# The head of a hybrid layer kernel: order of x, of the transposes and of the first two projection units

## Chip, cores and metric

The kernel runs on one core of one Trainium2 chip. The metric is device microseconds of one execution; the kernel before took 150.55 us as the median of three runs (150.08 to 150.64).

## What is computed

One DeepNorm layer over x of 256 rows and 1024 columns in float32. A first LayerNorm gives h. One projection takes h (1024 columns) to the inputs of four mixers (Mamba-2, HGRN2, retention, block attention); each mixer gives 256 columns, gated; an output projection takes their concatenation back to 1024 columns; a second LayerNorm takes 2^0.25 times h plus the result.

```python
h = _layernorm(x, emb_ln_g, emb_ln_b)
proj = einsum('bld,dn->bln', h, w_in)
q, f_raw, i, gate = the HGRN2 columns of proj
f = lb + (1 - lb) * sigmoid(f_raw)
...
y = einsum('blm,md->bld', y_cat, w_out)
out = _layernorm(2 ** 0.25 * h + y, ln_g, ln_b)
```

Only the head is touched here: the first LayerNorm, the transposition of h, and the projections `h_f` (the `f_raw` columns) and `h_q` (the `q` columns), with `h_i` behind them.

## The kernel before

**Layout.** x lies in two tiles of 128 rows, `xt0` and `xt1`. The normalised rows `xn` are transposed by TensorE in 16 blocks of 128 x 128 (8 column slices k, two row tiles T); slice k of both tiles shares one PSUM bank, and `h_in(k)` (line 307) evicts it with the LayerNorm's gain and bias, per partition, from the small table `ch`.

**Three products for one.** Every float32 operand is split into a high part, rounded to float32r by a cast (`whi`, `hhi`), and the rest (`wlo`, `hlo`, a subtraction on VectorE). A projection is the sum of hi x hi, hi x lo and lo x hi. `split_hi` (line 218) casts a weight tile on ScalarE, `split_lo` (line 227) makes its rest on VectorE. A unit is a group of 256 (or 260) columns; its weights come as two tiles j of four slices each, 512 KB a tile, so a unit is 8 slices x 3 products x 2 halves = 48 matmuls of 256 columns.

**Order.** The schedule is written out by hand: each engine executes its instructions in the order in which the program lists them, and waits where an input is not there. SP issues all loads in the order of the `load_w` calls (line 193); the tiles come from a ring of five buffers (`raw`), and a load into a buffer waits until `split_lo` has read what was in it. The mixers' steps are hung onto slots, two per unit: `begin(slot)` (line 1064) issues the load of three units ahead, the cast of two units ahead, the mixers' steps of the slot and the low part of two units ahead; then `project(slot)` issues the matmuls.

**The head, in its order.** SP: four half tiles of x (lines 159 to 162), the identity matrix out of the constants (line 165), the first unit's tile 0 in two pieces, `ch` (line 237), tile 1 in two pieces, the other constants, the second unit, two small tables, the third unit. TensorE: three matmuls on a tile of zeros (`WARM`, line 178). VectorE: statistics of each half tile (`ln_stats`, line 265), `ln_scale` (line 268: mean and variance, epsilon, and on POOL the power of -1/2), `lnb` = -mean x scale (line 288), which ScalarE's way of normalising takes as its bias. `ln_apply` (line 273) normalises in halves: three on VectorE, one on ScalarE. TensorE transposes slices 0 to 3 of tile 0, then of tile 1; `h_in` evicts them. `first_unit` (line 337) transposes one further slice ahead of each of its first four steps and multiplies slice by slice: hi x hi of slice k, then hi x lo of slice k - 1. The h_q unit's hi products come behind (`project(2, (0, 1))`), then the first unit's products with the low weights, then the second half of h_q, and in slots 2 and 3 its products with the low weights. Slot 4 is the first of `h_i`. `hgrn_gate` and `hgrn_key` (slots 0 and 1) take `h_f`, `hgrn_query` (slot 4) takes `h_q`.

`ldec` and `mm` (lines 714, 715) are two tiles of 1024 columns of the Mamba-2 mixer, which are free until its scores are made.

Of the kernel before, what the change touches and what calls it, by code (L numbers as in the profile page):

```python
# [17 lines left out]
P = 128  # L18
# [104 lines left out]
def hybrid_layer(  # L123
# [35 lines left out]
    for T in range(NT):  # L159
        for hf in range(2):  # L160
            nc.sync.dma_start(xt[T][:, hf * 512:hf * 512 + 512],
                              x[T * P:(T + 1) * P, hf * 512:hf * 512 + 512])
    ch = cp.tile([P, C_FREE], F32, name="ch")
    ck = cp.tile([P, K_FREE], F32, name="ck")
    nc.sync.dma_start(ck[:, :P], consts[:, :P])
# [6 lines left out]
    nc.gpsimd.memset(mhalf, -0.5)  # L172

# [4 lines left out]
    for _ in range(WARM):  # L178
        nc.tensor.matmul(wb, warm[:, :P], warm, start=True, stop=True)  # L179
# [13 lines left out]
    def load_w(i, j, parts=1):  # L193
# [10 lines left out]
        t = wp.tile(shape, F32, tag="raw", bufs=5, name=f"wr_{name}_{j}")  # L204
# [31 lines left out]
    load_w(0, 0, 2)  # L236
    nc.sync.dma_start(ch, chan)
    load_w(0, 1, 2)
    nc.sync.dma_start(ck[:, P:], consts[:, P:])
    for j in range(2):  # L240
        load_w(1, j)
# [4 lines left out]
    for j in range(2):  # L246
        load_w(2, j)
# [12 lines left out]
    lnb = sb([P, 1], "lnb")  # L260
# [7 lines left out]
    def ln_scale(T):  # L268
        nc.vector.bn_aggr(lmv[T], lst[T])
        (nc.gpsimd, nc.vector)[T].tensor_scalar(lrs[T], lmv[T][:, 1:2], LN_EPS, None, op0=ALU.add)  # L270
        nc.gpsimd.tensor_tensor(lrs[T], lrs[T], mhalf[:, :1], op=ALU.pow)

    def ln_apply(T, hf):
        cs = slice(hf * 512, hf * 512 + 512)
        if (T, hf) == (0, 1):
            nc.scalar.activation(xn[T][:, cs], xt[T][:, cs], AF.Identity, scale=lrs[T][:, 0:1],
                                 bias=lnb[:, 0:1])
            return
        nc.vector.tensor_scalar(xn[T][:, cs], xt[T][:, cs], lmv[T][:, 0:1], lrs[T][:, 0:1],  # L279
                                op0=ALU.subtract, op1=ALU.mult)  # L280

    ln_stats(0, 0)
    ln_stats(0, 1)
    ln_stats(1, 0)
    ln_scale(0)
    ln_stats(1, 1)
    ln_scale(1)
    nc.vector.scalar_tensor_tensor(lnb, lmv[0][:, 0:1], -1.0, lrs[0], op0=ALU.mult, op1=ALU.mult)
    split_hi(0, 0, 2, (0,))
    for hf in range(2):  # L290
        for T in range(NT):
            ln_apply(T, hf)
    split_hi(0, 0, 2, (1,))
    split_lo(0, 0, 2, (0,))
# [3 lines left out]
    trb = {}  # L298

    def h_transpose(k, T):  # L300
        if T == 0:
            trb[k] = bank(f"tr{k}")
        nc.tensor.transpose(trb[k][:, T * P:(T + 1) * P], xn[T][:, k * P:(k + 1) * P], ident)  # L303

    hfs = {}

    def h_in(k):
        hf = hfs[k] = sb([P, SEQ], f"hf{k}", tag="hf", bufs=4)
        g, b = ch[:, C_EG + k:C_EG + k + 1], ch[:, C_EB + k:C_EB + k + 1]
        if k == 0:  # L310
            nc.scalar.activation(hhi[:, k, :], trb[k][:, :SEQ], AF.Identity, scale=g, bias=b)
            nc.vector.tensor_scalar(hf, trb[k][:, :SEQ], g, b, op0=ALU.mult, op1=ALU.add)
            return
        nc.scalar.activation(hf, trb[k][:, :SEQ], AF.Identity, scale=g, bias=b)
        if k == KT - 1:
            nc.scalar.copy(hhi[:, k, :], hf)
        else:
            nc.vector.tensor_copy(hhi[:, k, :], hf)
# [818 lines left out]
```

## Time and profile before

| | before |
|---|---|
| median of three runs | 150.55 us |
| the profiled execution | 150.44 us |
| its span in the trace | 148.7 us |
| outside the span | 1.74 us |
| mean granted TensorE clock | 0.976 |
| TensorE busy | 136.5 us, 92% |
| VectorE busy | 116.6 us, 78% |
| ScalarE busy | 75.1 us, 50% |

Times in the trace run from the span's start. In its rows PE is TensorE's matmuls and PEld its weight loads (one ahead of each matmul), DVE is VectorE, ACT ScalarE, POOL GpSimd, and SPq the queue from which SP issues its DMAs. A row names the line, the operation, output<-inputs and the shapes; in brackets it says how long the engine was idle before it and what ended that. A float32 matmul or transpose stands in the trace as one record or as two.

### The profile page before, as it was taken

What the parts mean: (1) busy time and instruction counts of PE and PEld (TensorE: products, weight loads), DVE (VectorE), ACT (ScalarE), POOL (GpSimd) and SP (SyncE); (2) the same over time, 40 slices, a digit from 0 to 9 for tenths busy, and PEclk for the clock granted to TensorE, in tenths of its full rate; (3) what the DMA queues carried; (4) which work ended last, traced back from release to release, by engine and by line L of the source; (5) the groups of instructions that cost most, each with busy time, mean ns of one, the idle gap of its engine ahead of it and who ended that gap; (6) DMA issues with size and microseconds to landing.
All of it is one profiled execution on the core that took longest, in us unless ns stands there. A gap on an engine that the chain in (4) does not pass through costs nothing.

```text
span 148.7 us, 3074 instructions
## 1 busy us (share of the span) xinstructions
PE 136.5 (92%) x1224; PEld 122.2 (82%) x1224; DVE 116.6 (78%) x241; ACT 75.1 (50%) x122; POOL 17.8 (12%) x23
## 2 busy tenths in 40 slices
PE   5669999999999999999999999999999999999800
PEld 3159999999999998878899999999888888888800
DVE  2689977999596397969997599976969995378681
ACT  3079967752451859599709970054576635000000
POOL 4230000000000000000061018014002200004040
PEclk9969999999999999999999999999999999999995
DMA  4899289999858331694625820179773550000304
GB/s 157 265 387 361 68 283 363 294 294 356 228 156 253 129 84 57 156 267 163 179 86 145 315 110 4 35 238 382 247 233 93 180 155 0 0 0 0 141 0 141
DMA packets 9533, 26.05 MB, mean 175 GB/s; under 512 B 1072, under 2 KB 1968, under 8 KB 9264
## 3 DMA queue, kind: packets, MB, share of 16 engines
q1 hardware_dynamic: 9088, 25.35, 52.4%
q10 hardware_dynamic: 432, 0.52, 1.0%
q8 instruction: 9, 0.15, 0.4%
q14 instruction: 4, 0.03, 0.1%
HBM read 24.82 MB, written 1.05 MB: 174 GB/s over the span
## 4 chain that ended last, share of the span: by engine, by line
PE 82%; DVE 8%; DMA 3%; ACT 1%; SPq 1%; POOLq 1%; issue 1%; POOL 1%; DVEq 0%
PE pj_gg L381 8%; PE po L993 5%; PE po L994 5%; PE po L992 5%; PE pj_h_f L346 4%; PE pj_xs L420 4%; PE pj_m_k L420 4%; PE pj_m_g L420 4%; PE pj_r_k L420 4%; PE pj_m_q L420 4%; PE pj_h_i L420 4%; PE pj_zv L381 4%; PE pj_h_q L420 4%; PE pj_r_v L420 4%; PE pj_r_q L420 4%; DMA xt<-in_x_dram 3%
## 5 line engine op out<-in xcount | busy, mean ns | idle before, releaser
L992 PE MATMUL po<-whi_wo,yhi 128*128 128x512 f32 (+1 forms) x40 | 14.0, 350 | 0.0
L993 PE MATMUL po<-wlo_wo,yhi 128*128 128x512 f32 (+1 forms) x40 | 14.0, 349 | 0.0
L994 PE MATMUL po<-whi_wo,ylo 128*128 128x512 f32 (+1 forms) x40 | 13.9, 348 | 0.0
L225 ACT CAST whi_wo<-wr_wo 128x1024 fp32r<-128x1024 f32 x8 | 8.2, 1049 | 4.0 <-DMA wr_wo<-in_wo_dram 2.8
L234 DVE TENSOR_TENSOR wlo_wo<-wr_wo,whi_wo 128x1024 fp32r<-128x1024 f32 x8 | 9.6, 1218 | 0.0
L710 POOL TENSOR_SCALAR_AFFINE_SELECT ra<-ahi 128x1024 fp32r<-128x1024 f32 x1 | 1.1, 1101 | 64.5 <-DVE ahi L706 64.5
L992 PEld LDWEIGHTS po<-whi_wo,yhi 128*128 128x128 f32 x40 | 7.5, 188 | 1.1
L993 PEld LDWEIGHTS po<-wlo_wo,yhi 128*128 128x128 f32 x40 | 7.5, 188 | 1.0
L994 PEld LDWEIGHTS po<-whi_wo,ylo 128*128 128x128 f32 x40 | 7.5, 188 | 1.0
L225 ACT CAST whi_zv<-wr_zv 128x1024 fp32r<-128x1024 f32 x4 | 4.2, 1047 | 6.8 <-PE pj_xs L420 3.4
L656 DVE SCALAR_TENSOR_TENSOR cacc_xs<-pj_xs,ch,cacc_xs 128x255 f32<-128x255 f32 (+2 forms) x6 | 2.9, 482 | 4.7 <-ACT cacc_xs L654 4.6
L381 PE MATMUL pj_zv<-whi_zv,hhi 128*128 128x512 f32 x16 | 6.5, 406 | 0.0
L1000 DVE TENSOR_TENSOR xn<-xn,po 128x512 f32<-128x512 f32 (+1 forms) x5 | 2.9, 580 | 4.4 <-PE po L994 4.4
L381 PE MATMUL pj_gg<-whi_gg,hhi 128*128 128x512 f32 x16 | 6.4, 398 | 0.0
L381 PE MATMUL pj_zv<-whi_zv,hlo 128*128 128x512 f32 x16 | 6.3, 394 | 0.0
L381 PE MATMUL pj_gg<-whi_gg,hlo 128*128 128x512 f32 x16 | 6.3, 394 | 0.0
L381 PE MATMUL pj_zv<-wlo_zv,hhi 128*128 128x512 f32 x16 | 6.3, 392 | 0.0
L381 PE MATMUL pj_gg<-wlo_gg,hhi 128*128 128x512 f32 x16 | 6.3, 392 | 0.0
L303 PE MATMUL tr<-ck,xn 128*128 128x128 f32 x16 | 3.8, 384 | 2.6 <-DVE xn L279 2.6
L179 PE MATMUL warm<-warm 128*128 128x512 f32 x6 | 4.5, 914 | 1.5 <-DVE warm L176 1.5
L303 PEld LDWEIGHTS tr<-ck,xn 128*128 128x128 f32 x16 | 2.7, 197 | 3.7 <-DVE xn L279 3.7
L225 ACT CAST whi_gg<-wr_gg 128x1024 fp32r<-128x1024 f32 x4 | 4.2, 1045 | 2.5 <-DMA wr_gg<-in_w_dram 1.7
(281 smaller groups left out, 490.7 us busy)
## 6 DMA issues: line engine op xcount, KB each, us to landing
wr_wo<-in_wo_dram SPq DMA_DIRECT2D x8, 512.0 KB, 3.8
wr_zv<-in_w_dram SPq DMA_DIRECT2D x4, 512.0 KB, 4.7
rb<-in_rows_dram SPq DMA_DIRECT2D x2, 1024.0 KB, 7.1
wr_gg<-in_w_dram SPq DMA_DIRECT2D x4, 512.0 KB, 4.7
wr_h_i<-in_w_dram SPq DMA_DIRECT2D x2, 520.0 KB, 4.9
xt<-in_x_dram SPq DMA_DIRECT2D x4, 256.0 KB, 3.8
wr_h_f<-in_w_dram SPq DMA_DIRECT2D x4, 256.0 KB, 5.2
wr_h_q<-in_w_dram SPq DMA_DIRECT2D x2, 512.0 KB, 5.6
```

The source lines that it names most:

```text
L179: nc.tensor.matmul(wb, warm[:, :P], warm, start=True, stop=True)
L225: copy(whi[i, j][:, r, :], t[:, r, :])
L234: nc.vector.tensor_sub(wlo[i, j][:, r, :], t[:, r, :], whi[i, j][:, r, :].bitcast(F32))
L303: nc.tensor.transpose(trb[k][:, T * P:(T + 1) * P], xn[T][:, k * P:(k + 1) * P], ident)
L346: nc.tensor.matmul(ps[n], l[:, n * P:(n + 1) * P], r[:, k, :], start=(k == 0 and q == 0), stop=(k == KT - 1 and q == 2))
L381: nc.tensor.matmul(ps_of[name, T], l[:, k, ts], r, start=(k == 0 and q == 0), stop=(k == KT - 1 and q == 2))
L420: nc.tensor.matmul(ps, l, r, start=(n == 0), stop=(n == len(seq) - 1))
L656: nc.vector.scalar_tensor_tensor(a_[:, d:], ps[:, :SEQ - d], tap(3 - d), a_[:, d:], op0=ALU.mult, op1=ALU.add)
L992: nc.tensor.matmul(po[T, c0], yhi[:, k, ts], hi, start=(i == 0 and j == 0), stop=False)
L993: nc.tensor.matmul(po[T, c0], yhi[:, k, ts], lo, start=False, stop=False)
L994: nc.tensor.matmul(po[T, c0], ylo[:, k, ts], hi, start=False, stop=(i == 3 and j == 1))
L1000: nc.vector.tensor_add(xn[T][:, cs], xn[T][:, cs], po[T, cs.start])
```

## The change

The first row tile of x is loaded in halves as before, the second as one transfer of whole rows, and `ch` is issued from ScalarE's queue ahead of everything. The identity is made on POOL instead of loaded. Both tiles' scales are computed on VectorE with POOL's power; `lnb` stands between the statistics of the second tile's halves. ScalarE normalises all of tile 0 in two halves, VectorE all of tile 1 in four quarters. TensorE transposes all eight slices of tile 0, then runs one more matmul on zeros (`keep_warm(1)`), then six slices of tile 1. Two slices now share a bank.

`first_units` multiplies the units h_f and h_q side by side, slice by slice, h_q one slice behind, and then both with their low weights. The weight casts of both units are placed between the evictions by a table (`CASTS`). The first unit's weights lie in the mixer tiles `mm` and `ldec` instead of the ring. The loads' order is both units' tile 0, both units' tile 1, the third unit, then constants and tables. Casts and low parts of the third unit move to slot 0, all ahead of `hgrn_key`.

```diff
@@ -156,13 +156,12 @@
     xt = [sb([P, DM], f"xt{T}") for T in range(NT)]
-    for T in range(NT):
-        for hf in range(2):
-            nc.sync.dma_start(xt[T][:, hf * 512:hf * 512 + 512],
-                              x[T * P:(T + 1) * P, hf * 512:hf * 512 + 512])
     ch = cp.tile([P, C_FREE], F32, name="ch")
+    nc.scalar.dma_start(ch, chan)
+    for T, st in ((0, 512), (1, DM)):
+        for c in range(0, DM, st):
+            nc.sync.dma_start(xt[T][:, c:c + st], x[T * P:(T + 1) * P, c:c + st])
     ck = cp.tile([P, K_FREE], F32, name="ck")
-    nc.sync.dma_start(ck[:, :P], consts[:, :P])
     ident = ck[:, K_ID:K_ID + P]
     tri = ck[:, K_TRI:K_TRI + P]
     one2 = ck[:, K_ONE2:K_ONE2 + 2]
@@ -170,13 +169,23 @@
     mhalf = cp.tile([P, 8], F32, name="mhalf")
     nc.gpsimd.memset(mhalf, -0.5)
+    nc.gpsimd.memset(ident, 1.0)
+    nc.gpsimd.affine_select(out=ident, in_=ident, pattern=[[1, P]], compare_op=ALU.is_equal, fill=0.0,
+                            base=0, channel_multiplier=-1)
+
+    lnb = sb([P, 1], "lnb")
+    nc.scalar.copy(lnb, mhalf[:, 0:1])
     warm = sb([P, 512], "warm", tag="att")
     nc.vector.memset(warm, 0.0)
     wb = bank("warm")
-    for _ in range(WARM):
-        nc.tensor.matmul(wb, warm[:, :P], warm, start=True, stop=True)
+
+    def keep_warm(n):
+        for _ in range(n):
+            nc.tensor.matmul(wb, warm[:, :P], warm, start=True, stop=True)
+
+    keep_warm(WARM)
     e1 = sb([P, 2, SEQ], "e1")
     nc.gpsimd.memset(e1, 0.0)
@@ -201,7 +210,9 @@
             b = int(name[2:])
             shape = [P, 2, 512]
             src = wo[:, 2 * b:2 * b + 2, j * 512:j * 512 + 512]
-        t = wp.tile(shape, F32, tag="raw", bufs=5, name=f"wr_{name}_{j}")
+
+        t = (sb(shape, f"wr_{name}_{j}", tag=("mm", "ldec")[j]) if i == 0 else
+             wp.tile(shape, F32, tag="raw", bufs=5, name=f"wr_{name}_{j}"))
         st = shape[1] // parts
         for q in range(parts):
             r = slice(q * st, (q + 1) * st)
@@ -233,18 +244,16 @@
             r = slice(q * st, (q + 1) * st)
             nc.vector.tensor_sub(wlo[i, j][:, r, :], t[:, r, :], whi[i, j][:, r, :].bitcast(F32))
-    load_w(0, 0, 2)
-    nc.sync.dma_start(ch, chan)
-    load_w(0, 1, 2)
+    for j in range(2):
+        for i in range(2):
+            load_w(i, j)
+    for j in range(2):
+        load_w(2, j)
     nc.sync.dma_start(ck[:, P:], consts[:, P:])
-    for j in range(2):
-        load_w(1, j)
     lev = cp.tile([P, 5, 64], I32, name="lev")
     nc.sync.dma_start(lev, lev_tab)
     rw = cp.tile([P, R_SMALL], F32, name="rw")
     nc.sync.dma_start(rw, rows[:, 0:R_SMALL].to_broadcast([P, R_SMALL]))
-    for j in range(2):
-        load_w(2, j)
     def row(n):
         o, c = ROFF[n]
@@ -267,55 +275,57 @@
     def ln_scale(T):
         nc.vector.bn_aggr(lmv[T], lst[T])
-        (nc.gpsimd, nc.vector)[T].tensor_scalar(lrs[T], lmv[T][:, 1:2], LN_EPS, None, op0=ALU.add)
+        nc.vector.tensor_scalar(lrs[T], lmv[T][:, 1:2], LN_EPS, None, op0=ALU.add)
         nc.gpsimd.tensor_tensor(lrs[T], lrs[T], mhalf[:, :1], op=ALU.pow)
-
-    def ln_apply(T, hf):
-        cs = slice(hf * 512, hf * 512 + 512)
-        if (T, hf) == (0, 1):
-            nc.scalar.activation(xn[T][:, cs], xt[T][:, cs], AF.Identity, scale=lrs[T][:, 0:1],
-                                 bias=lnb[:, 0:1])
-            return
-        nc.vector.tensor_scalar(xn[T][:, cs], xt[T][:, cs], lmv[T][:, 0:1], lrs[T][:, 0:1],
-                                op0=ALU.subtract, op1=ALU.mult)
     ln_stats(0, 0)
     ln_stats(0, 1)
+    ln_scale(0)
     ln_stats(1, 0)
-    ln_scale(0)
+    nc.vector.scalar_tensor_tensor(lnb, lmv[0][:, 0:1], -1.0, lrs[0], op0=ALU.mult, op1=ALU.mult)
     ln_stats(1, 1)
     ln_scale(1)
-    nc.vector.scalar_tensor_tensor(lnb, lmv[0][:, 0:1], -1.0, lrs[0], op0=ALU.mult, op1=ALU.mult)
-    split_hi(0, 0, 2, (0,))
-    for hf in range(2):
-        for T in range(NT):
-            ln_apply(T, hf)
-    split_hi(0, 0, 2, (1,))
-    split_lo(0, 0, 2, (0,))
+    for c in range(0, DM, 512):
+        nc.scalar.activation(xn[0][:, c:c + 512], xt[0][:, c:c + 512], AF.Identity,
+                             scale=lrs[0][:, 0:1], bias=lnb[:, 0:1])
+    for c in range(0, DM, 256):
+        nc.vector.tensor_scalar(xn[1][:, c:c + 256], xt[1][:, c:c + 256], lmv[1][:, 0:1],
+                                lrs[1][:, 0:1], op0=ALU.subtract, op1=ALU.mult)
+    split_hi(0, 0, 2)
     hhi = cp.tile([P, KT, SEQ], F32R, name="hhi")
     hlo = cp.tile([P, KT, SEQ], F32R, name="hlo")
-    trb = {}
+
+    trp = [bank(f"tr{j}").rearrange("p (k t) -> p k t", k=2) for j in range(5)]
+    trb = [trp[(k + 1) // 2][:, (k + 1) % 2, :] for k in range(KT)]
     def h_transpose(k, T):
-        if T == 0:
-            trb[k] = bank(f"tr{k}")
         nc.tensor.transpose(trb[k][:, T * P:(T + 1) * P], xn[T][:, k * P:(k + 1) * P], ident)
+    for k in range(KT):
+        h_transpose(k, 0)
+    keep_warm(1)
+    for k in range(6):
+        h_transpose(k, 1)
     hfs = {}
+    CASTS = {1: ((1, 0), (0,)), 4: ((0, 1), (0,)), 5: ((0, 1), (1,)), 6: ((1, 1), (0,)),
+             7: ((1, 1), (1,))}
+
     def h_in(k):
-        hf = hfs[k] = sb([P, SEQ], f"hf{k}", tag="hf", bufs=4)
+        hf = hfs[k] = sb([P, SEQ], f"hf{k}", tag="hf", bufs=6)
         g, b = ch[:, C_EG + k:C_EG + k + 1], ch[:, C_EB + k:C_EB + k + 1]
+        t = trb[k]
         if k == 0:
-            nc.scalar.activation(hhi[:, k, :], trb[k][:, :SEQ], AF.Identity, scale=g, bias=b)
-            nc.vector.tensor_scalar(hf, trb[k][:, :SEQ], g, b, op0=ALU.mult, op1=ALU.add)
+            nc.scalar.activation(hhi[:, k, :], t, AF.Identity, scale=g, bias=b)
+            nc.vector.tensor_scalar(hf, t, g, b, op0=ALU.mult, op1=ALU.add)
             return
-        nc.scalar.activation(hf, trb[k][:, :SEQ], AF.Identity, scale=g, bias=b)
-        if k == KT - 1:
-            nc.scalar.copy(hhi[:, k, :], hf)
-        else:
-            nc.vector.tensor_copy(hhi[:, k, :], hf)
+        nc.scalar.activation(hf, t, AF.Identity, scale=g, bias=b)
+        if k in CASTS:
+            split_hi(*CASTS[k][0], 2, CASTS[k][1])
+        nc.vector.tensor_copy(hhi[:, k, :], hf)
+        if k == 3:
+            split_hi(1, 0, 2, (1,), nc.vector.tensor_copy)
         h_rest(k - 1)
         if k == KT - 1:
             h_rest(k)
@@ -323,49 +333,40 @@
     def h_rest(k):
         nc.vector.tensor_sub(hlo[:, k, :], hfs[k], hhi[:, k, :].bitcast(F32))
-    for k in range(4):
-        h_transpose(k, 0)
-    for k in range(4):
-        h_transpose(k, 1)
-    for k in range(4):
+    for k in range(6):
         h_in(k)
-    split_hi(0, 1, 2, (0,))
     ps_of, hq = {}, {}
-    def first_unit():
-
-        ps = [bank(f"pj_h_f{n}")[:, :SEQ] for n in range(2)]
-        ps_of["h_f", 0], ps_of["h_f", 1] = ps
-
-        def part(k, q):
-            l = (whi, whi, wlo)[q][0, k // 4][:, k % 4]
+    def first_units():
+
+        ps = [[bank(f"pj_{names[i]}{n}")[:, :SEQ] for n in range(2)] for i in range(2)]
+        for n in range(2):
+            ps_of["h_f", n], hq[n] = ps[0][n], ps[1][n]
+
+        def part(i, k, q):
+            l = (whi, whi, wlo)[q][i, k // 4][:, k % 4]
             r = (hhi, hlo, hhi)[q]
             for n in range(2):
-                nc.tensor.matmul(ps[n], l[:, n * P:(n + 1) * P], r[:, k, :], start=(k == 0 and q == 0),
-                                 stop=(k == KT - 1 and q == 2))
-        for k in range(KT):
-            if k < 4:
-                h_transpose(k + 4, 0)
-                h_transpose(k + 4, 1)
-                h_in(k + 4)
-            if k == 1:
-                split_hi(0, 1, 2, (1,), nc.vector.tensor_copy)
-            part(k, 0)
-            if k:
-                part(k - 1, 1)
-        part(KT - 1, 1)
-        split_lo(0, 0, 2, (1,))
-        split_lo(0, 1, 2)
-        split_hi(1, 0)
-        split_hi(1, 1)
-        project(2, (0, 1))
-        for k in range(KT):
-            part(k, 2)
-        project(3, (0, 1))
-
-    def project(slot, parts=(0, 1, 2)):
+                nc.tensor.matmul(ps[i][n], l[:, n * P:(n + 1) * P], r[:, k, :],
+                                 start=(k == 0 and q == 0), stop=(k == KT - 1 and q == 2))
+        for k in range(KT + 2):
+            for i, d, q in ((0, 0, 0), (0, 1, 1), (1, 1, 0), (1, 2, 1)):
+                if 0 <= k - d < KT:
+                    part(i, k - d, q)
+            if k == 0:
+                for k_ in (6, 7):
+                    h_transpose(k_, 1)
+                for k_ in (6, 7):
+                    h_in(k_)
+        for i in range(2):
+            for j in range(2):
+                split_lo(i, j)
+            for k in range(KT):
+                part(i, k, 2)
+
+    def project(slot):
         i, j = divmod(slot, 2)
         name = names[i]
@@ -384,14 +385,11 @@
         def wk(k):
             hi = whi[i, k // 4][:, k % 4]
-            return hi, wlo[i, k // 4][:, k % 4] if 2 in parts else hi
+            return hi, wlo[i, k // 4][:, k % 4]
         if name in CHAN:
-            if name == "h_q":
-                if j not in hq:
-                    hq[j] = bank(f"pj_h_q{j}")[:, :SEQ]
-            elif j == 0:
+            if j == 0:
                 ps_of[name] = pp.tile([P, 2, SEQ], F32, tag="pp", name=f"pj_{name}")
-            ps = hq[j] if name == "h_q" else ps_of[name][:, j, :]
+            ps = ps_of[name][:, j, :]
             cs = slice(j * P, (j + 1) * P)
             def trip(k):
@@ -412,12 +410,11 @@
                 hi, lo = wk(k)
                 return (hhi[:, k, ts], hi), (hlo[:, k, ts], hi), (hhi[:, k, ts], lo)
         seq = [(k, q) for k in range(KT) for q in range(3)]
-        if slot < 4:
+        if slot < 6:
             seq.sort(key=lambda kq: kq[1] == 2)
         for n, (k, q) in enumerate(seq):
-            if q in parts:
-                l, r = trip(k)[q]
-                nc.tensor.matmul(ps, l, r, start=(n == 0), stop=(n == len(seq) - 1))
+            l, r = trip(k)[q]
+            nc.tensor.matmul(ps, l, r, start=(n == 0), stop=(n == len(seq) - 1))
     yhi = cp.tile([P, KT, SEQ], F32R, name="yhi")
     ylo = cp.tile([P, KT, SEQ], F32R, name="ylo")
@@ -1064,21 +1061,24 @@
     def begin(slot):
         if slot < 32:
             load_w(*divmod(slot + 6, 2))
-        if slot < 34:
+        if slot == 0:
+            for j in range(2):
+                split_hi(2, j)
+            for j in range(2):
+                split_lo(2, j)
+        elif 1 < slot < 34:
             split_hi(*divmod(slot + 4, 2))
         for st in steps.get(slot, []):
             st()
-        if slot < 34:
+        if 1 < slot < 34:
             split_lo(*divmod(slot + 4, 2))
-    first_unit()
+    first_units()
     lower_bound()
-    for q in (2, 3):
-        split_lo(*divmod(q, 2))
     for slot in range(s0):
         begin(slot)
-        if slot > 1:
-            project(slot, (2,) if slot < 4 else (0, 1, 2))
+        if slot > 3:
+            project(slot)
     order = [(i, T, n) for i, T in ((0, 0), (1, 0), (0, 1), (2, 0), (3, 0))
              for n in range(len(OCOLS[T]) - 1)]
     order += [(i, 1, n) for n in range(len(OCOLS[1]) - 1) for i in range(1, 4)]
```

## Rows read from the trace of the kernel before

**Rows 1.** The page, busy us, share of the span and instructions of each engine

```profile
PE 136.5 (92%) x1224; PEld 122.2 (82%) x1224; DVE 116.6 (78%) x241; ACT 75.1 (50%) x122; POOL 17.8 (12%) x23
```

**Rows 2.** TensorE's waits over the whole span: us in total, times, longest

```profile
PE lv L582 <- DVE F L528: 0.2, 1, 0.2
```

**Rows 3.** Timeline, TensorE: start us, us, engine, line, what [idle before]

```profile
10.85 0.77 PE L346 MATMUL pj_h_f<-hhi,whi_h_f 128*128 128x256 f32 x2
...
18.01 1.94 PEld L346 LDWEIGHTS pj_h_f<-hhi,wlo_h_f 128*128 128x128 f32 x16
...
19.88 0.19 PEld L420 LDWEIGHTS pj_h_q<-hhi,whi_h_q 128*128 128x128 f32 x1
...
23.76 0.28 PE L420 MATMUL pj_h_i<-whi_h_i,hhi 128*128 128x260 f32 x1
```

**Rows 4.** Timeline, TensorE, the transposes

```profile
8.66 2.53 PE L303 MATMUL tr<-ck,xn 128*128 128x128 f32 x10 [2.63 <-DVE xn L279]
...
9.65 1.14 PEld L303 LDWEIGHTS tr<-ck,xn 128*128 128x128 f32 x6 [0.28 <-DVE xn L279]
...
12.18 0.24 PEld L303 LDWEIGHTS tr<-ck,xn 128*128 128x128 f32 x2
```

**Rows 5.** Timeline of the head, the other engines

```profile
0.79 1.80 SPq L161 DMA_DIRECT2D xt<-in_x_dram  x4
...
6.96 0.69 DVE L266 BATCH_NORM_STATS2 lst<-xt 128x6 f32<-128x512 f32 x1 [0.46 <-DMA xt<-in_x_dram]
...
8.00 0.15 DVE L288 SCALAR_TENSOR_TENSOR lnb<-lmv,lrs 128x1 f32<-128x1 f32 x1
...
8.16 0.86 POOL L271 TENSOR_TENSOR lrs<-lrs,mhalf 128x1 f32<-128x1 f32 x1 [0.69 <-DVE lnb L288]
...
8.23 0.62 ACT L225 CAST whi_h_f<-wr_h_f 128x512 fp32r<-128x512 f32 x1 [6.16 <-DMA wr_h_f<-in_w_dram]
...
8.75 0.81 ACT L276 ACTIVATE xn<-xt,lnb,lrs 128x512 f32<-128x512 f32 x1
...
9.05 1.00 DVE L279 TENSOR_SCALAR xn<-xt,lmv,lrs 128x512 f32<-128x512 f32 x2 [0.45 <-POOL lrs L271]
...
9.47 0.60 ACT L225 CAST whi_h_f<-wr_h_f 128x512 fp32r<-128x512 f32 x1
...
10.16 0.56 ACT L311 ACTIVATE hhi<-tr,ch 128x256 fp32r<-128x256 f32 x1
...
10.63 1.47 ACT L314 ACTIVATE hf<-tr,ch 128x256 f32<-128x256 f32 x3
...
11.43 0.42 DVE L324 TENSOR_TENSOR hlo<-hf,hhi 128x256 fp32r<-128x256 f32 x1
...
11.77 0.28 DVE L318 CAST hhi<-hf 128x256 fp32r<-128x256 f32 x1
...
17.80 2.36 DVE L234 TENSOR_TENSOR wlo_h_q<-wr_h_q,whi_h_q 128x1024 fp32r<-128x1024 f32 x2
```

**Rows 6.** Stretches: length, busy us of PE, PEld, DVE, ACT, POOL, granted clock, DMA share, GB/s

```profile
6.00:6.50 0.50, 0.04 (x1) 0.00 (x0) 0.50 (x2) 0.00 (x0) 0.00 (x0) 1.00 0.99 305
...
8.00:8.50 0.50, 0.00 (x0) 0.00 (x0) 0.50 (x3) 0.27 (x1) 0.34 (x1) 0.85 1.06 399
8.50:11.50 3.00, 2.84 (x13) 2.57 (x14) 2.45 (x7) 2.91 (x6) 0.81 (x2) 0.50 1.04 392
...
11.50:12.00 0.50, 0.50 (x5) 0.50 (x4) 0.50 (x4) 0.50 (x3) 0.00 (x0) 0.73 0.91 366
```

**Rows 7.** DMA issues: count, KB each, median us from issue to landing

```profile
wr_r_q<-in_w_dram SPq DMA_DIRECT2D x2, 512.0 KB, 3.8
...
ch<-in_chan_dram SPq DMA_DIRECT2D x1, 19.0 KB, 5.1
```

**Rows 8.** The page, costliest groups, an affine_select on POOL

```profile
L710 POOL TENSOR_SCALAR_AFFINE_SELECT ra<-ahi 128x1024 fp32r<-128x1024 f32 x1 | 1.1, 1101 | 64.5 <-DVE ahi L706 64.5
```

**Rows 9.** Timeline, TensorE's weight loads of the warm-up matmuls

```profile
4.23 0.34 PEld L179 LDWEIGHTS warm<-warm 128*128 128x128 f32 x1 [0.52 <-issue]
```

More of the change, by code (lines that the diff above doesn't have):

```diff
@@ L259, in hybrid_layer @@
     lmv = [sb([P, 2], f"lmv{T}") for T in range(NT)]
-    lnb = sb([P, 1], "lnb")
     lrs = [sb([P, 1], f"lrs{T}") for T in range(NT)]
```

## The prediction

> **What bounds the kernel now.** The page first: TensorE is busy 92% of the span, VectorE 78%, ScalarE 50% [rows 1]. Then TensorE's waits: behind the head it waits once more for another engine, 0.2 us [rows 2]. So from about 12 us to 136 us the time is matmuls in a row, and a change of the head is worth what it moves the first matmul behind both head units, the first of `h_i`, now at 23.76 us [rows 3]. I call that point M; everything behind it keeps its length, so the change is M after less M before. In the head the reader should see three limits. The transposes start at 8.66 us after a wait of 2.63 for `xn`, because the last quarter of x is read at 6.96 [rows 4, 5]. The granted clock: TensorE goes idle just after 6.0 us, the clock falls between 8.0 and 8.5 (mean 0.85 there), stays at 0.50 and comes back in 11.5 to 12 (mean 0.73) [rows 6]. From there the two units' matmuls run almost without a gap, 16 in 1.87 us [rows 3].
>
> **x first.** The four quarters were issued from 0.79 us in 1.80, some 0.46 apart, and the fourth, issued near 2.17, was read at 6.96, 4.8 later [rows 5]. Now the second tile is one transfer at the third place, 1.70 us. Bounds for its landing L: 512 KB tiles with little queued land in 3.8 us [rows 7], so 5.5 us; or no sooner than now, 6.96. The fourth quarter's 4.8 would give 6.5. I take the middle of the bounds, 6.25. The identity no longer comes by DMA: a memset and an affine_select of 128 columns on POOL; an affine_select of 1024 took 1.10 us [rows 8], so both are done by some 3 us while x is on its way; uncovered they would cost at most 2 us. `ch` (19 KB, 5.1 us to landing [rows 7]) moves from SP's queue to ScalarE's, ahead of x; the first to want it is the eviction at 10.16 [rows 5]. By the Trainium skill (DMA: Bandwidth & Descriptors, "Queues, rings and completion order") an engine takes turns between the queues that have work for it, so `ch` would travel beside x rather than behind it; no row of before has two queues busy here.
>
> **LayerNorm.** VectorE now stands at the statistics of the second tile before it writes `lnb`, and both ScalarE halves of `xn[0]` wait for `lnb`: L + 0.69 + 0.15 + 0.81 and 0.05 of hand-over [rows 5], so the first half is there at L + 1.7 = 7.95 and the second 0.72 later (8.75 to 9.47), 8.7. Meanwhile VectorE does the second statistics, aggregate and epsilon, and POOL the power, 0.86; `xn` began at 9.05, 2.1 after the last read [rows 5]. One statistics more (0.69) now follows L, so the quarters of `xn[1]` begin at L + 2.8 = 9.05, and the first is there at 9.35 (two halves took 1.00).
>
> **Transposes and the keep-warm.** Transposes issue every 0.19 us at half clock (6 weight loads in 1.14) and every 0.12 at full (2 in 0.24) [rows 4]. Tile 0's first four start at 7.95, the other four end at 9.2 (full) or 9.45 (half). Then comes the keep-warm matmul, and tile 1's transposes are queued behind it. The three warm-up matmuls made six records, so one costs two; records lay 0.86 apart early on (a weight load of 0.34 with 0.52 idle ahead of it [rows 9]), which is the pace of the lower level (1.2 GHz) although the column granted shows 1.00 there. So 1.71 at half clock and 0.86 at full. Tile 1 starts at 10.05 or 11.15; `xn[1]` has long been ready, so the keep-warm lies on the path. The first eviction began 0.5 after tile 1's first transpose at half clock (9.65 to 10.16 [rows 4, 5]), some 0.35 at full. Call its start A: 10.4 or 11.65, against 10.16 now.
>
> **Two units side by side.** Behind A, TensorE has all 96 matmuls of both units at 0.117 [rows 3], 11.25 us, and two transposes, 0.24. It starts 0.69 after A (10.16 to 10.85) and waits some 0.45 more for the second `hhi` and the first `hlo`: A + 12.65. ScalarE has evictions every 0.49 (three in 1.47) and, moved between them, five weight casts at 0.52 (8.23 to 8.75) [rows 5]; four stand before the last eviction, done at A + 0.5 + 7 x 0.49 + 4 x 0.52 + 0.1 = A + 6.1. TensorE asks for that slice at A + 1.4 + 7 x 0.94 = A + 8.0, so the casts are hidden; they would cost up to 2.5 uncovered. VectorE then has the last `hhi` and two `hlo`, 0.2 + 0.34 + 0.42 [rows 5], ends at A + 7.1, and makes four low parts in a row, 1.18 each (2.36 for two): A + 8.3, 9.5, 10.6, 11.8. TensorE reaches them at A + 8.9, 9.8, 10.8, 11.7. They are just in time, so M = A + 12.7. Before, M lay 13.6 behind A, with half clock and waits inside. The gain at equal A is 0.9; A = 11.05 breaks even.
>
> **Weights and what stands behind.** The first unit's weights go into mixer tiles, so the ring of five raw buffers begins with the second unit and SP issues further ahead. TensorE had no wait for that: nothing. On ScalarE the first unit's casts stand ahead of the first eviction and must begin by 9.3. Their 512 KB are next in line behind x, with the other unit's half behind them; in the old order, behind 64 KB more, the first 256 KB were cast at 8.23, as they landed, and the next at 9.47 without a wait [rows 5]. So landing is at 8.2 to 9.5, and I take 8.7: little cover, up to 0.2 lost. Behind M, VectorE reaches `hgrn_query` some 0.8 us later than now, since two `h_i` low parts moved ahead of `hgrn_key`; TensorE's one wait on VectorE is 0.2 us in 100 [rows 2], so I cost it at nothing, at most 0.8.
>
> **Sum.** At full clock A = 10.4 and M = 23.1, 0.66 before 23.76. The profiled execution took 150.44 us, so 149.8; the median of the runs is 0.11 higher: 149.9.
>
> **Rivals.**
> *Low clock, slower.* The clock fell between 8.0 and 8.5 us, with TensorE idle from 6.0 [rows 6]. Transposes now resume at 7.95; whether that forestalls the fall is open. If it falls all the same and is back only near 11.7, the keep-warm costs 1.71 on the path: A = 11.65, M = 24.35, 0.6 slower, 151.1, and with L = 6.96 as well 151.8. It decides where the clock is half when the keep-warm begins, about 9.4. For it: most of the idle stretch is still there. Against it: the stretch is 0.7 shorter. The Trainium skill (TensorE: Matmul & The Clock Gate, "Part 4: PE-mode transpose") says that the full clock does not engage in transpose mode; by that this rival would be certain. The trace does not agree: transposes at 12.18 issued at full pace, at a granted 1.00 [rows 4, 6], and the clock rose behind ten transposes and a few matmuls.
> *x no sooner.* All of tile 1 is waited for now, with weights behind it on the queue: L = 6.96, A = 11.1, M = 23.8, no change, 150.5.
> *x much sooner.* L = 5.5, as an unhindered tile: A = 9.65, M = 22.35, 149.1.
> *No saving.* If VectorE's row of low parts slips by 0.9, M - A stays 13.6, and the first case gives 150.8; I count it with x no sooner.
>
> **How the numbers follow.** Forecast case 0.42, low clock 0.30, x no sooner or no saving 0.14, x much sooner 0.14. A measurement of this kernel can tell 0.5% from no change, 0.75 us: 149.8 and 151.3. The forecast lies at that bound, so a little under half of it counts as faster (0.20) and 0.22 as same; low clock is mostly slower (0.18), for a smaller L same (0.12); x no sooner is 0.06 same and, with a clock that falls on top, 0.08 slower; much sooner is all faster. That is 0.34 faster, 0.40 same, 0.26 slower. The range runs from a little under the much-sooner case, 148.8, to the low clock with a middling L, 151.4.
>
> **What would show it.** Right: the second tile's statistics begin near 6.25, transposes near 8.0; the granted clock is 1.00 from 9 to 12 or back before 10; the keep-warm's records are 0.43 long in pitch; the first eviction is near 10.4, the first `h_i` matmul near 23.1, and no new TensorE wait over 0.3 us stands behind it. Wrong: keep-warm records 0.86 apart and a first eviction near 11.6; statistics at 7 us; ScalarE waiting for `wr_h_f` past 9.3; a new wait of TensorE for `wlo_h_q`, or for `qk` near 32 us.

## The result and the profile after

The changed kernel takes 156.66 us as the median of six executions (155.43 to 157.41), the kernel before 150.44 (150.08 to 150.64, six as well). The ratio is 1.041, 95% interval 1.037 to 1.045: slower by 6.2 us, where 0.5 less was forecast. Ratios, here and below, are formed from the executions near each kernel's fastest; where a kernel's executions fall into two groups, the median and the range say more, and both are given.

The page, against [rows 1]: TensorE is busy 4 us longer in a span 7.0 longer. The second row is its granted clock in the 40 slices of the span, in tenths of full speed.

```profile
PE 140.5 (90%) x1226; PEld 125.0 (80%) x1226; DVE 116.8 (75%) x242; ACT 75.4 (48%) x125; POOL 17.9 (12%) x24
...
PEclk9968559999999999999999999999999999999996
```

TensorE's waits, over the whole span. Before, one wait of 2.6 stood ahead of the first transpose and 0.2 behind the head [rows 2, 4]. Now there are two in the head, and the second is for ScalarE's `hf`, an eviction:

```profile
PE tr L303 <- ACT xn L289: 3.1, 1, 3.1
PE tr L303 <- ACT hf L323: 2.8, 1, 2.8
```

The timeline of the head (start, length, engine, line, what, and in brackets the idle time before it and what ended it) has the whole story; it answers to [rows 3 to 5].

```profile
7.92 0.69 DVE L274 BATCH_NORM_STATS2 lst<-xt 128x6 f32<-128x512 f32 x1 [1.83 <-DMA xt<-in_x_dram]
...
8.71 1.52 ACT L289 ACTIVATE xn<-xt,lnb,lrs 128x512 f32<-128x512 f32 x2 [6.01 <-DVE lnb L285]
...
9.58 1.97 PE L303 MATMUL tr<-ck,xn 128*128 128x128 f32 x8 [3.05 <-ACT xn L289]
...
11.34 1.73 PE L186 MATMUL warm<-warm 128*128 128x512 f32 x2
...
12.90 0.82 PE L303 MATMUL tr<-ck,xn 128*128 128x128 f32 x6
...
13.21 0.57 ACT L320 ACTIVATE hhi<-tr,ch 128x256 fp32r<-128x256 f32 x1 [1.95 <-PE tr L303]
...
13.84 0.50 PE L352 MATMUL pj_h_f<-hhi,whi_h_f 128*128 128x256 f32 x2
...
16.50 0.60 ACT L323 ACTIVATE hf<-tr,ch 128x256 f32<-128x256 f32 x1
...
17.16 0.69 PE L303 MATMUL tr<-ck,xn 128*128 128x128 f32 x2 [2.82 <-ACT hf L323]
...
20.20 0.63 PE L352 MATMUL pj_h_q<-hlo,whi_h_q 128*128 128x256 f32 x2
...
20.63 0.63 PE L352 MATMUL pj_h_f<-hhi,whi_h_f 128*128 128x256 f32 x2
...
31.10 0.28 PE L417 MATMUL pj_h_i<-whi_h_i,hhi 128*128 128x260 f32 x1
```

The second tile's statistics begin at 7.92, not near 6.25. The first transpose is at 9.58, the keep-warm's two records take 1.73, and the first eviction (A) starts at 13.21 against 10.16 before. Then TensorE does two matmuls at 13.84 and stands until 17.16 for a transpose that waits for an eviction which ended at 17.10. Behind it, pairs of matmuls follow each other every 0.43 us (20.20 to 20.63), 1.8 times the 0.235 of two at 0.117 [rows 3]. The first `h_i` matmul (M) is at 31.10, 7.34 later than before, and the span is 7.0 longer: all of the loss is ahead of M. Stretches of the same trace (length, busy us of PE, PEld, DVE, ACT, POOL, granted clock, DMA share, GB/s) show what the wait did to the clock:

```profile
9.00:10.00 1.00, 0.42 (x2) 0.42 (x3) 0.64 (x3) 1.00 (x2) 0.21 (x1) 0.67 1.02 418
12.50:13.00 0.50, 0.50 (x2) 0.10 (x1) 0.00 (x0) 0.00 (x0) 0.00 (x0) 0.75 1.01 416
...
16.00:16.50 0.50, 0.00 (x0) 0.00 (x0) 0.50 (x3) 0.50 (x2) 0.49 (x1) 0.66 0.51 202
16.50:22.50 6.00, 5.34 (x25) 5.35 (x26) 5.30 (x13) 5.93 (x10) 0.06 (x1) 0.50 0.03 12
22.50:23.00 0.50, 0.50 (x5) 0.50 (x4) 0.50 (x1) 0.43 (x1) 0.00 (x0) 0.51 0.00 0
```

It fell between 9 and 10 in TensorE's first idle stretch, came back at about 12.75, fell again in the second between 16.0 and 16.5, and stayed at half until almost 23. So M - A is 17.9 us, where 12.7 was forecast and 13.6 was measured before.

### The profile page after: what moved, and what is told of

Same layout as the page of the kernel before. It is cut to its first block, busy times and chain, and to the rows that moved or that the text cites. A ratio compares the mean times of both kernels' runs of the same rounds, so it can differ in the third digit from the quotient of the medians.

```text
span 155.7 us, 3073 instructions
## 1 busy us (share of the span) xinstructions
PE 140.5 (90%) x1226; PEld 125.0 (80%) x1226; DVE 116.8 (75%) x242; ACT 75.4 (48%) x125; POOL 17.9 (12%) x24
## 4 chain that ended last, share of the span: by engine, by line
PE 80%; DVE 7%; ACT 4%; DMA 4%; issue 1%; POOLq 1%; SPq 1%; POOL 0%; DVEq 0%
PE pj_gg L382 7%; PE po L990 5%; PE po L991 5%; PE po L989 5%; PE pj_h_f L352 4%; PE pj_h_q L352 4%; DMA xt<-in_x_dram 4%; PE pj_xs L417 4%; PE pj_m_k L417 4%; PE pj_m_g L417 4%; PE pj_r_k L417 4%; PE pj_m_q L417 4%; PE pj_h_i L417 4%; PE pj_zv L382 4%; PE pj_r_v L417 4%; PE pj_r_q L417 4%
## 5 line engine op out<-in xcount | busy, mean ns | idle before, releaser
L186 PE MATMUL warm<-warm 128*128 128x512 f32 x8 | 6.8, 995 | 1.5 <-DVE warm L181 1.5
L274 DVE BATCH_NORM_STATS2 lst<-xt 128x6 f32<-128x512 f32 x4 | 2.7, 692 | 4.7 <-DMA xt<-in_x_dram 4.7
```

## The experiments

All but g1 and h2 are the changed kernel with an edit; f1 to f5 have the edits of e2 as well. Times are medians, with the range and the number of executions. L is the start of the statistics of the second tile's first half (and second half). L and the columns behind it are of the profiled execution of each kernel, the last column is its time.

| kernel | us | L | first transpose | A | M | M - A | profiled us |
|---|---|---|---|---|---|---|---|
| before | 150.44 | 5.70, 6.96 | 8.66 | 10.16 | 23.76 | 13.6 | 150.44 |
| after | 156.66 | 7.92, 8.60 | 9.58 | 13.21 | 31.10 | 17.9 | 157.41 |
| e1 all ahead | 152.02 (149.37 to 152.86, 10) | 8.21, 8.88 | 9.87 | 13.47 | 26.42 | 12.95 | 152.86 |
| e2 own bank | 152.42 (149.56 to 152.61, 10) | 6.22, 6.89 | 7.87 | 10.24 | 23.12 | 12.9 | 149.56 |
| e3 no keep-warm | 154.67 (154.44 to 155.52, 4) | 7.57, 8.24 | 9.22 | 11.30 | 28.11 | 16.8 | 154.44 |
| e4 halves | 152.71 (151.20 to 154.12, 10) | 5.99, 6.66 | 7.64 | 10.01 | 27.82 | 17.8 | 154.12 |
| f1 bank, halves | 149.19 (148.90 to 150.89, 6) | 6.22, 6.91 | 7.88 | 11.66 | 24.55 | 12.9 | 150.89 |
| f2 bank, halves, no keep-warm | 148.43 (148.24 to 151.27, 4) | 5.47, 6.35 | 7.19 | 8.98 | 21.91 | 12.9 | 148.28 |
| f3 bank, no keep-warm | 150.70 (148.86 to 151.70, 10) | 7.76, 8.43 | 9.41 | 11.63 | 25.32 | 13.7 | 151.70 |
| f4 bank, halves, warm-up of 4 | 149.46 (149.00 to 149.76, 7) | 6.13, 7.73 | 7.96 | 10.36 | 23.25 | 12.9 | 149.62 |
| f5 as f4, no keep-warm | 148.77 (148.26 to 150.40, 10) | 5.46, 7.94 | 8.01 | 10.57 | 23.46 | 12.9 | 149.83 |
| g1 before, warm-up of 5 | 150.29 (149.49 to 150.60, 10) | 5.44, 7.27 | 8.98 | 10.34 | 23.94 | 13.6 | 150.59 |
| h1 halves, no keep-warm, shared bank | 152.69 (150.82 to 154.37, 10) | 5.43, 7.24 | 7.26 | 9.91 | 27.88 | 18.0 | 154.18 |
| h2 before, second tile whole | 151.09 (150.35 to 152.12, 10) | 6.28, 7.00 | 8.77 | 9.76 | 24.05 | 14.3 | 150.61 |

Executions of the kernel before beside them: 150.32 (e1 to e4), 150.17 (f1 to f4), 150.51 (f5, g1, h1, h2).

**What holds TensorE at 14 to 17 us.** Theory: slices 5 and 6 share a bank, so writing slice 6 waits for the reading of slice 5. Rivals: the matmuls would wait for the evictions anyway, or the place in the order alone is at fault. e1 moves the two late transposes ahead of the evictions:

```diff
-    for k in range(6):
+    for k in range(KT):
         h_transpose(k, 1)
@@
-                for k_ in (6, 7):
-                    h_transpose(k_, 1)
```

> All eight transposes of the second row tile are issued ahead of the evictions, instead of six there and two inside the first step of the two units. In the trace of the changed kernel the seventh stands 2.8 us for the eviction of slice 5, because slices 5 and 6 share a bank, and all matmuls of the units stand behind it; the granted clock then falls to half from 16.2 to 22.9 us. Theory (the shared bank holds TensorE, and the idle stretch costs the clock): the wait is gone, the clock stays up, the first h_i matmul comes 12.7 to 13.5 us after the first eviction instead of 17.9, and the time is 151.5 to 152.5 us. Rival (the matmuls would have waited anyway, for ScalarE's evictions with the casts between them): TensorE waits for hhi instead, and the time stays within 1 us of 156.7.

e2 leaves the order and places the slices 0 | 1 2 | 3 4 | 5 | 6 7 instead of 0 | 1 2 | 3 4 | 5 6 | 7:

```diff
-    trb = [trp[(k + 1) // 2][:, (k + 1) % 2, :] for k in range(KT)]
+    trb = [trp[(0, 1, 1, 2, 2, 3, 4, 4)[k]][:, (0, 0, 1, 0, 1, 0, 0, 1)[k], :] for k in range(KT)]
```

> The order of the changed kernel is kept; only the placing of the slices in the five banks differs: 0 alone, 1 with 2, 3 with 4, 5 alone, 6 with 7. Theory (shared bank): slice 6 no longer waits for the eviction of slice 5, so 151.5 to 152.5 us, the same as with all transposes ahead. Rival (the place in the order alone holds TensorE): 156 us or more, as in the changed kernel, while the run with all transposes ahead is fast.

Measured: 152.02 and 152.42 us; ratios to before 1.0015 (0.9965 to 1.0065) and 1.0024 (0.9949 to 1.0098), with executions that spread over 3 us. Both are some 4.4 us faster than the changed kernel, and in both M - A is about 12.9. In e2's timeline the same transpose, at the same place in the order, starts 0.96 after the first eviction without a wait:

```profile
7.87 1.36 PE L303 MATMUL tr<-ck,xn 128*128 128x128 f32 x8 [1.85 <-ACT xn L289]
...
10.24 0.57 ACT L320 ACTIVATE hhi<-tr,ch 128x256 fp32r<-128x256 f32 x1 [0.69 <-PE tr L303]
...
11.20 0.38 PE L303 MATMUL tr<-ck,xn 128*128 128x128 f32 x2
...
23.12 0.28 PE L417 MATMUL pj_h_i<-whi_h_i,hhi 128*128 128x260 f32 x1
```

```profile
8.00:9.00 1.00, 0.95 (x8) 0.71 (x9) 0.33 (x2) 1.00 (x3) 0.56 (x1) 1.00 1.03 369
```

So it is the bank, and both rivals fall. (Slices that share a bank are also parts of one tile of the program, and no run parts the two. The trace shows TensorE waiting for ScalarE; whether the chip would need that wait is not shown.) e2's profiled execution is also the forecast case nearly line by line: statistics at 6.22 (6.25 forecast), transposes at 7.87 (7.95), A 10.24 (10.4), M 23.12 (23.1), 149.56 us (149.8). But only one of its ten executions ran so; the others lie at 151.8 to 152.6, with a mean granted clock of 0.968 to 0.976 against 0.990. e1's profiled execution, at 152.86, looks like these: the same loads, read at 8.21, with the clock at half when the keep-warm begins:

```profile
8.21 0.69 DVE L274 BATCH_NORM_STATS2 lst<-xt 128x6 f32<-128x512 f32 x1 [2.66 <-DMA xt<-in_x_dram]
...
11.63 1.69 PE L186 MATMUL warm<-warm 128*128 128x512 f32 x2
...
13.47 0.56 ACT L320 ACTIVATE hhi<-tr,ch 128x256 fp32r<-128x256 f32 x1 [1.92 <-PE tr L303]
```

```profile
9.00:10.00 1.00, 0.13 (x1) 0.14 (x2) 0.93 (x3) 1.00 (x2) 0.00 (x0) 0.78 1.06 430
...
12.00:13.00 1.00, 1.00 (x2) 0.23 (x1) 0.05 (x1) 0.00 (x0) 0.00 (x0) 0.52 1.04 425
```

**The keep-warm matmul.** e3 takes `keep_warm(1)` out of the changed kernel.

> The changed kernel without the keep-warm matmul between the two tiles' transposes. Theory (it lies on the path: 1.73 us at half clock, and the second tile's transposes begin at 12.2 to 12.9 although xn is ready from 10.8): the first eviction begins 1.0 to 1.7 us earlier, at 11.5 to 12.2; the wait for slice 5 stays, so the time falls by about as much, to 155 to 155.7 us. Rival (it brings the clock back, from 12.75 us on): without it the clock comes back later, and the time is 156.5 us or more.

154.67 us, 2.0 less, a little more than the theory had. A is 11.30 in the profiled execution, 1.9 earlier; 0.35 of that is x, which was read at 7.57. The wait for slice 5 stays (2.5 us). The rival falls: the clock is back at about 13 us without the matmul too (granted 0.97 from 13 to 14).

**x in halves.** e4 loads the second tile as before:

```diff
-    for T, st in ((0, 512), (1, DM)):
+    for T, st in ((0, 512), (1, 512)):
```

> The changed kernel with the second row tile of x loaded in halves, as before. Theory (waiting for one whole tile makes the statistics late: 7.92 us against 5.6 and 6.96 before): the first half's statistics begin by 6 us and the second's near 7.2, the first eviction moves 0.7 to 1 us earlier, and the time falls to 155.5 to 156 us. Rival (the weights issued behind x take its bandwidth, in whatever pieces x comes): the last half is still read near 7.9, the scale of the first tile alone is earlier, and the time stays within 0.3 us of 156.7.

152.71 us, 3.95 less, four times what was expected. The rows say why: VectorE writes `lnb` behind the first half's statistics alone, so ScalarE normalises tile 0 from 6.77 instead of 8.71, and the transposes start at 7.64 instead of 9.58. That shortens TensorE's idle stretch as well: the clock is still 1.00 when the keep-warm runs (1.02 instead of 1.73), and falls only in the wait for the bank. In this profile the last half was early too (6.66). That it is the first half which counts is seen in h1, f4 and f5 below: their last halves were read at 7.24 to 7.94, and yet ScalarE begins at 6.39 to 7.09.

```profile
6.77 1.52 ACT L289 ACTIVATE xn<-xt,lnb,lrs 128x512 f32<-128x512 f32 x2 [4.07 <-DVE lnb L285]
...
7.64 1.37 PE L303 MATMUL tr<-ck,xn 128*128 128x128 f32 x8 [1.10 <-ACT xn L289]
...
8.84 1.02 PE L186 MATMUL warm<-warm 128*128 128x512 f32 x2
...
13.95 0.69 PE L303 MATMUL tr<-ck,xn 128*128 128x128 f32 x2 [2.81 <-ACT hf L323]
```

```profile
9.00:10.00 1.00, 1.00 (x6) 0.47 (x5) 0.83 (x3) 0.66 (x2) 0.00 (x0) 1.00 1.01 406
...
11.00:12.00 1.00, 0.14 (x2) 0.00 (x0) 0.70 (x3) 1.00 (x4) 0.00 (x0) 1.00 1.03 424
12.00:13.00 1.00, 0.00 (x0) 0.00 (x0) 0.96 (x4) 1.00 (x4) 0.00 (x0) 0.89 1.01 413
13.00:14.00 1.00, 0.05 (x1) 0.05 (x1) 1.00 (x4) 1.00 (x3) 0.00 (x0) 0.50 1.01 390
```

**Both repairs, and the keep-warm again.** f1 has the edits of e2 and e4, f2 that of e3 too, f3 those of e2 and e3.

> Own bank for slices 6 and 7 (as e2) and the second row tile in halves (as e4). With the own bank alone the executions lie in two groups, near 149.6 and near 152.4 us, and the profiled one of 149.56 read the second tile at 6.22 us and kept the full clock, while with all transposes ahead the tile was read at 8.21, the clock fell and the time was 152.86. Theory (what is left is the landing of the whole tile, and the clock that falls when it is late): in halves the last statistics begin by 6.7 us in every execution, the keep-warm matmul starts before 9 us at full clock, and nearly all executions lie at 149.2 to 150.0 us. Rival (the two groups come from the clock alone, whenever x lands): two groups remain, median 151 to 152.5 us.

> As f1, without the keep-warm matmul between the tiles. Theory (it lies on the path and costs 0.86 us at full clock, 1.7 at half): 0.4 to 0.9 us faster than f1, 148.4 to 149.4 us. Rival (it keeps the clock up): without it the granted clock falls between 9 and 13 us in most executions, and the time is 150 us or more.

> Own bank, the second tile as one transfer, no keep-warm matmul. Theory (keep-warm on the path, at half clock in most executions where the tile lands late): the slow group of e2 (152.4 us) moves by 1 to 1.7 us, median 150.7 to 151.5 us. Rival (keep-warm brings the clock back): no faster than e2, 152 us or more.

f1: 149.19 us, ratio to before 0.9927 (0.9904 to 0.9950); five of six executions at 148.9 to 149.4, where the theory had 149.2 to 150.0, and one at 150.89. That one is the profiled one, and it misses the theory's signs: the last statistics begin at 6.91, the transposes start at 7.88, as in e2, but the clock falls at once, and the keep-warm begins only at 9.49 and takes 1.92.

```profile
7.88 1.82 PE L303 MATMUL tr<-ck,xn 128*128 128x128 f32 x8 [1.90 <-ACT xn L289]
...
9.49 1.92 PE L186 MATMUL warm<-warm 128*128 128x512 f32 x2
...
11.66 0.56 ACT L320 ACTIVATE hhi<-tr,ch 128x256 fp32r<-128x256 f32 x1 [2.10 <-PE tr L303]
```

```profile
8.00:9.00 1.00, 1.00 (x6) 0.72 (x7) 0.33 (x2) 1.00 (x3) 0.56 (x1) 0.62 1.04 414
9.00:10.00 1.00, 1.00 (x5) 0.83 (x4) 1.00 (x4) 0.57 (x2) 0.00 (x0) 0.50 1.00 397
```

f2: 148.43 us, ratio 0.9872 (0.9840 to 0.9904), 0.76 below f1 and the lowest median of all, though of four executions only, and one of them took 151.27 at a mean clock of 0.975. Without the keep-warm the clock stays at 1.00 in the profiled execution, so the rival falls for that one. f3: 150.70, 1.7 below e2, as its theory had it. The quickest executions differ by 0.7 in both pairs (148.90 and 148.24; 149.56 and 148.86). So the keep-warm is on the path, and costs most where the clock is low.

```profile
6.32 1.52 ACT L289 ACTIVATE xn<-xt,lnb,lrs 128x512 f32<-128x512 f32 x2 [3.61 <-DVE lnb L285]
...
7.19 2.51 PE L303 MATMUL tr<-ck,xn 128*128 128x128 f32 x14 [1.03 <-ACT xn L289]
...
8.98 0.56 ACT L319 ACTIVATE hhi<-tr,ch 128x256 fp32r<-128x256 f32 x1
...
21.91 0.28 PE L416 MATMUL pj_h_i<-whi_h_i,hhi 128*128 128x260 f32 x1
```

**A longer warm-up.** f4 is f1 with `WARM = 4`, f5 is f2 with it.

> As f1, with four warm-up matmuls instead of three, so that TensorE is busy to about 7.3 us and idle for 0.3 us instead of 1.1 before the first transpose. Theory (the idle stretch ahead of the transposes decides whether the clock falls): all executions lie within 0.5 us of each other at 149.0 to 149.6 us. Rival (the clock does not depend on it, or the fourth matmul at half clock runs into the transposes): same as f1 or up to 0.9 us slower.

> Own bank, halves, no keep-warm, four warm-up matmuls ahead of x. Theory (the keep-warm between the tiles lies on the path; warm-up ahead of x does not, and it shortens the idle stretch that costs the clock): 148.2 to 148.8 us in all executions, without the single slow ones (151.27) of the version with three. Rival (the fourth warm-up matmul runs into the first transposes, or the clock falls all the same for want of the matmul between the tiles): 149 us or more, or two groups.

f4: 149.46 us, and seven executions within 0.8 us of each other (the theory had 0.5), against 2.0 in f1: none stands apart, though the median is no better. f5: 148.77, ratio 0.9905 (0.9872 to 0.9938), with executions up to 150.40; its profiled one (149.83) kept the clock at 1.00 throughout, and was late because the last half of x was read at 7.94 and the first tile-1 transpose waited 1.15 for `xn`. Its first transposes, too, stand behind the fourth warm-up matmul: they start 1.58 after ScalarE begins `xn`, against 0.87 in e2. So not every long execution is the clock's, and f5's theory of 148.8 in all executions is missed. For the clock the mean values lean its way: all seventeen executions of f4 and f5 have a mean clock of 0.982 or above, while one of six of f1 and one of four of f2 lie at 0.974 and 0.975. That is too few to call it shown.

```profile
7.94 0.69 DVE L274 BATCH_NORM_STATS2 lst<-xt 128x6 f32<-128x512 f32 x1 [1.54 <-DMA xt<-in_x_dram]
...
9.74 1.38 DVE L292 TENSOR_SCALAR xn<-xt,lmv,lrs 128x256 f32<-128x256 f32 x4 [0.67 <-POOL lrs L279]
...
10.20 1.09 PE L303 MATMUL tr<-ck,xn 128*128 128x128 f32 x6 [1.15 <-DVE xn L292]
```

**The clock and the whole tile in the kernel before.** g1 is the kernel before with `WARM = 5`; h2 is the kernel before with the second tile as one transfer.

> The kernel before with five warm-up matmuls instead of three, and nothing else. Theory (the low clock from 8.3 to 11.7 us costs the old kernel too): the granted clock stays up, the transposes issue at 0.12 us instead of 0.19, and the time falls by 0.3 to 1.0 us, to 149.4 to 150.0 us; that much of the gain has nothing to do with the change. Rival (the old head is paced by the evictions, so the clock costs it nothing): within 0.2 us of before.

> The kernel before with the second row tile of x in one transfer of whole rows, and nothing else. Theory (a whole tile is read later than its last half, since every byte of it is waited for while the weights issued behind it move as well): its statistics begin at 7 us or later for both halves, the transposes start 0.7 us or more later than 8.66, and the time rises by 0.5 to 1.5 us. Rival (only the weights in longer rows and ch on ScalarE's queue made it late): the statistics begin by 6.5 us, and the time is within 0.3 us of before.

g1: 150.29 against 150.51, ratio 0.9977 (0.9952 to 1.0001). The clock is up from 8 to 12 us, and M - A is still 13.6. The 0.22 by the medians lies between the rival's bound and the theory's, but M - A speaks for the rival: the low clock from 8.3 to 11.7 cost the old head next to nothing.

```profile
8.00:9.00 1.00, 0.02 (x1) 0.03 (x1) 0.89 (x4) 0.86 (x2) 0.52 (x1) 1.00 1.05 392
9.00:10.00 1.00, 0.66 (x5) 0.42 (x5) 0.63 (x2) 0.98 (x2) 0.33 (x1) 1.00 1.06 372
10.00:11.00 1.00, 0.89 (x7) 0.65 (x7) 1.00 (x3) 0.66 (x2) 0.26 (x1) 1.00 1.06 342
```

h2: 151.09, 0.6 above before by the medians, ratio 1.0020 (0.9994 to 1.0046): inconclusive. The profiled execution read the whole tile at 6.28, so a whole tile need not be late; one profile does not say how often it is. In this one the clock fell only between 10 and 11 and was back at 14, and M - A is 14.3, with ScalarE waiting 0.60 for the last transposes: there a low clock seems to have cost the old head something. Over all profiles a whole tile was read at 6.22 to 8.21, the first of two halves at 5.43 to 6.22 and the last at 6.35 to 7.94: all scatter, and what made them scatter was not found.

**The bank alone, in the best surroundings.** h1 is f2 with slices 5 and 6 in one bank again.

> The changed kernel in halves and without the keep-warm, with slices 5 and 6 still in one bank: it differs from f2 (148.43 us) by the bank alone. Theory (the wait for slice 5 holds all matmuls some 2.5 to 2.8 us, and the clock falls in it in some executions): 2.5 to 4.5 us slower than f2, 151 to 153 us. Rival (the bank mattered only where the clock fell): under 1.5 us slower than f2.

152.69 us, 4.3 above f2, about the same as between e2 and the changed kernel (4.2). The wait in the row is 2.5. In this execution the clock had fallen before it, between 9 and 10, and came back only between 19 and 20. But two executions of h1 kept a mean clock of 0.984 (150.82 and 151.54), as three of f2 did (0.983 to 0.991, 148.24 to 148.58). Between these the difference is 2.8 on average, about the wait itself, so the rival falls; what the medians show beyond it goes with the clock.

```profile
9.91 0.56 ACT L319 ACTIVATE hhi<-tr,ch 128x256 fp32r<-128x256 f32 x1 [0.28 <-PE tr L303]
...
13.85 0.69 PE L303 MATMUL tr<-ck,xn 128*128 128x128 f32 x2 [2.48 <-ACT hf L322]
```

```profile
9.00:10.00 1.00, 0.49 (x3) 0.37 (x4) 0.96 (x3) 0.72 (x3) 0.00 (x1) 0.83 0.99 406
...
19.00:20.00 1.00, 1.00 (x7) 1.00 (x6) 1.00 (x2) 0.63 (x1) 0.00 (x0) 0.55 0.00 0
```

## Why the prediction was wrong

- **What bounds the kernel**: right. M moved by 7.34 and the span by 7.0; in every trace the span behind M is 124.6 to 125.0 us.
- **x first**: the landing was mis-sized. 6.25 was taken from bounds of 5.5 and 6.96; whole tiles were read at 6.22 to 8.21. The upper bound was wrong: four of the six were read later than 6.96. Why is open; the weights are issued earlier and in longer rows behind x, but no run shows that this is the reason. In the result's trace the miss is 1.67 us. That e2's 6.22 agrees with 6.25 is luck: it is the earliest of the six.
- **LayerNorm**: the chain behind L was right (first transpose at L + 1.66, forecast 1.7). What was read in it but not weighed is that both `xn[0]` halves hang on `lnb`, and `lnb` on the second tile: with x in halves the medians fall by 3.95 (e4) and 3.2 (f1 against e2).
- **Transposes and the keep-warm**: right in both cases. At full clock A was L + 4.0 (e2), forecast 4.15; at half L + 5.3 (after, e1), forecast 5.4. Taking it out gave 2.0, 1.7 and 0.8 us (e3, f3, f2).
- **Two units side by side**: here the prediction failed. The step said "Behind A, TensorE has all 96 matmuls of both units at 0.117 [rows 3], 11.25 us, and two transposes, 0.24." It priced the two late transposes as TensorE's work and did not ask what they wait for. Slice 6 was newly placed in the bank of slice 5, whose eviction is the sixth in ScalarE's queue, behind two casts; the transpose waited for it, 2.82 us, with every matmul of both units queued behind. The clock fell in that idle stretch, and 16.5 to 22.5 us at half go with the other 2.2 of the 5.0 us by which M - A is longer than in e2. Shown by e1, e2 and h1: by the medians 4.2 to 4.6 us of the 6.2. The Trainium skill (PSUM — Partial Sum Buffer, "PSUM bank collisions raise a hardware error") asks that PSUM be guarded by semaphore per bank and quadrant, not per address. The traces agree in so far as the program's wait goes by the bank: other columns, and yet a wait of 2.5 to 2.8 us, gone when the slice got another bank. With that wait away the rest of the step was right, 12.9 against 12.7; and ScalarE's casts were hidden, as forecast.
- **Half clock inside the old M - A**: it was there, but cost nothing. g1 has the clock up and the same 13.6. The side-by-side saves 0.7 at equal A, forecast 0.9.
- **Weights and what stands behind**: right. In e4, f4, f5 and h1 ScalarE's casts waited for the first unit's weights, at the latest until 9.19, but the first eviction then waited for a transpose. Behind M the changed kernel and its versions take 124.6 to 124.7, before 124.9.
- **The rivals**: "low clock" came true, in the changed kernel and, by the mean clock, in nine of ten executions of e2. It was priced right: f1's profiled execution, with x at 6.22 and a low clock, has A at 11.66 (11.65 forecast), M at 24.55 (24.35) and 150.89 us (151.1). With the bank repaired alone the kernel lies at 152.4, beyond even the 151.8 forecast for a low clock with L = 6.96; in e1 and f3, whose profiles show it, a tile read at 8.21 and 7.76 and a low clock come together. No rival held a wait between ScalarE's evictions and the transposes, and the range ended at 151.4.

## What to carry to other kernels

When tiles are packed two to a PSUM bank, list for each bank who reads and who writes it in program order: here a write placed behind a read of its neighbour waited for that read, and everything behind it on TensorE waited too. Price a moved instruction by what it may wait for, then by its duration. An idle stretch of TensorE may have to be charged twice, once as the stretch and once for the clock behind it. Both were paid after 2.8 us in the changed kernel; e2, after 1.85, paid only the first, and f1, after 1.90, both. And where one small result (here `lnb`) gates half of the work, look at which transfer stands ahead of it. Loading x in halves brought it forward here; moving `lnb` itself ahead of the second tile's statistics was not tried.

## What had not been expected

- Executions of one kernel differ by up to 3.5 us (e1, h1). Two things vary between the profiles: when x is read (6.22 in e2 and, of the same loads, 8.21 in e1) and whether the clock falls. In e2 and f1 TensorE went idle at about 6.0 and resumed at 7.87 and 7.88; in e2 the clock stayed at 1.00 and in f1 it fell between 8 and 9. What decides it stays open.
- After the fall at 16.0 to 16.5 the clock did not come back before 22.5, though TensorE was busy from 17.16 on. In e1 a fall between 9 and 10 was over by 13. In e3 the clock rose at about 13, while TensorE stood idle, and fell again at about 16.5, after it had been at work since 15.24.
- The low clock from 8.3 to 11.7 cost the old kernel next to nothing (g1, at most 0.5% by its interval), where the prediction had named it inside the 13.6 that the change was to shorten.
